# A fused add and GELU: from 1 MB tiles with stores on GpSimd's queue to uniform 512 KB chunks, x kept in SBUF, adds on GpSimd and temporaries in PSUM

## The chip, the cores and the metric

The kernel runs on one core of a Trainium2 chip. The metric is the device time of one execution in microseconds, as the median of several runs. One further execution was recorded by the hardware profiler; all views of the profile come from it.

## The reference

```python
x, y = randn(1024, 4096), randn(1024, 4096)      # float32
z = x + y
out = 0.5 * z * (1 + tanh(sqrt(2 / pi) * (z + 0.044715 * z ** 3)))   # float32
```

Two arrays of 16 MiB are read and one of 16 MiB is written: 48 MiB (50.33 MB) pass between HBM and SBUF. Each output element depends on one element of each input.

## The kernel before

The 1024 rows are viewed as 128 partitions with 8 rows each, so that one partition owns 32768 elements in a row, 128 KB of HBM. This row is cut along its length into 15 tiles of 2048 columns (1 MB for all partitions, 8 KB per partition) and a tail of 1024, 512, 256, 128 and 128 columns: 20 tiles.

For each tile, in the names of the code: `do_load` fetches a and b (lines 67 and 68, both from SyncE's queue, SP); `do_add` makes z = a + b on VectorE (DVE, line 75); `do_sq` makes w = k3 z² on ScalarE (ACT, line 81); `do_stt` makes w = (w + k1) z on VectorE (line 90); `do_ti` runs Tanh and then 0.5 w + 0.5 as an Identity, both on ScalarE (lines 100 and 105); `do_mul_store` makes w = z w on VectorE (line 116) and stores it from GpSimd's queue (POOL, line 117).

One loop at the end sets the order: in step t it emits the load of tile t, Tanh and Identity of t-3, the add of t-1, the second VectorE operation of t-2, the Square of t-1, and the product and store of t-3. The input pool has six buffers for each of a and b, the chain pool five for each of z and w. So a load waits for the add that read its buffer six tiles ago.

Of the kernel before, what the change touches and what calls it, by code (L numbers as in the profile page):

```python
# [1 line left out]

# [1 line left out]

# [4 lines left out]


@with_exitstack
def kernel(
    ctx: ExitStack,
    tc: tile.TileContext,
    x: bass.AP,
    y: bass.AP,
    out: bass.AP,
):
    nc = tc.nc  # L20
    P = nc.NUM_PARTITIONS
    fp32 = mybir.dt.float32

    N, D = x.shape
    assert N % P == 0
    rows_per_part = N // P

    k1 = math.sqrt(2.0 / math.pi)
    k3 = k1 * 0.044715
    sqrt_k3 = math.sqrt(k3)  # L30

    xv = x.rearrange("(p n) d -> p (n d)", p=P)
    yv = y.rearrange("(p n) d -> p (n d)", p=P)
    ov = out.rearrange("(p n) d -> p (n d)", p=P)

    total_free = rows_per_part * D
    FMAX = 2048

    tail = [1024, 512, 256, 128, 128]
    nbody = (total_free - sum(tail)) // FMAX  # L40
    assert sum(tail) + nbody * FMAX == total_free
    sizes = [FMAX] * nbody + tail
    offsets = []
    off = 0
    for F in sizes:
        offsets.append(off)
        off += F
    C = len(sizes)

    in_pool = ctx.enter_context(tc.tile_pool(name="inputs", bufs=6))  # L50
    chain_pool = ctx.enter_context(tc.tile_pool(name="chain", bufs=5))
    consts = ctx.enter_context(tc.tile_pool(name="consts", bufs=1))

    half = consts.tile([P, 1], fp32, tag="half")
    nc.vector.memset(half, 0.5)  # L55

    a_t: list = [None] * C
    b_t: list = [None] * C
    z_t: list = [None] * C
    w_t: list = [None] * C  # L60

    def do_load(c):
        F = sizes[c]
        sl = slice(offsets[c], offsets[c] + F)
        a = in_pool.tile([P, F], fp32, tag="a")
        b = in_pool.tile([P, F], fp32, tag="b")
        nc.sync.dma_start(out=a, in_=xv[:, sl])  # L67
        nc.sync.dma_start(out=b, in_=yv[:, sl])
        a_t[c] = a
        b_t[c] = b  # L70

    def do_add(c):
        F = sizes[c]
        z = chain_pool.tile([P, F], fp32, tag="z")
        nc.vector.tensor_add(out=z, in0=a_t[c], in1=b_t[c])  # L75
        z_t[c] = z

    def do_sq(c):
        F = sizes[c]
        w = chain_pool.tile([P, F], fp32, tag="w")  # L80
        nc.scalar.activation(  # L81
            out=w,
            in_=z_t[c],
            func=mybir.ActivationFunctionType.Square,
            scale=sqrt_k3,
        )
        w_t[c] = w

    def do_stt(c):
        nc.vector.scalar_tensor_tensor(  # L90
            out=w_t[c],
            in0=w_t[c],
            scalar=k1,
            in1=z_t[c],
            op0=mybir.AluOpType.add,
            op1=mybir.AluOpType.mult,
        )

    def do_ti(c):
        nc.scalar.activation(  # L100
            out=w_t[c],
            in_=w_t[c],
            func=mybir.ActivationFunctionType.Tanh,
        )
        nc.scalar.activation(  # L105
            out=w_t[c],
            in_=w_t[c],
            func=mybir.ActivationFunctionType.Identity,
            scale=0.5,
            bias=half,  # L110
        )

    def do_mul_store(c):
        F = sizes[c]
        sl = slice(offsets[c], offsets[c] + F)
        nc.vector.tensor_mul(out=w_t[c], in0=z_t[c], in1=w_t[c])  # L116
        nc.gpsimd.dma_start(out=ov[:, sl], in_=w_t[c])  # L117

    for t in range(C + 4):
        if 0 <= t < C:  # L120
            do_load(t)
        if 0 <= t - 3 < C:
            do_ti(t - 3)
        if 0 <= t - 1 < C:
            do_add(t - 1)
        if 0 <= t - 2 < C:
            do_stt(t - 2)
        if 0 <= t - 1 < C:
            do_sq(t - 1)
        if 0 <= t - 3 < C:  # L130
            do_mul_store(t - 3)


# [1 line left out]
_INS = ['x', 'y']  # L135
_OUTS = [((1024, 4096), 'float32')]


# [23 lines left out]
```

## Time and profile before

| | |
|---|---|
| median of 5 runs | 132.49 us (132.36 to 132.89) |
| the profiled execution's own time | 132.47 us |
| its span in the profile | 130.7 us |
| DVE busy | 107.8 us (83% of the span), 61 instructions |
| ACT busy | 96.0 us (73%), 61 instructions |
| POOL busy | 11.0 us (8%), 24 instructions |
| HBM read, written | 33.55 MB, 16.78 MB |
| packets | 8258; loads take 62.2% of the 16 engines' span, stores 30.9% |
| one 128x2048 operation | 2291 ns (L75), 1907 ns (L81), 2288 ns (L90), 1908 ns (L100), 2001 ns (L105), 2289 ns (L116) |
| one 128x1024 operation | 1222 ns (L75), 1041 ns (L81), 1224 ns (L90), 1039 ns (L100), 1132 ns (L105), 1225 ns (L116) |
| the issue of one store on POOL | 540 ns |

The span is the time between the first and the last instruction that the profiler recorded; the execution takes 1.8 us more. The page's second part shows the busy share of each engine and of the 16 DMA engines in 40 slices of 3.27 us. The view by stretches gives the same for stretches of one's own choice, and the GB/s that the DMA moved in each. The share of the DMA can come out somewhat above 1, because packets on one engine can overlap.

### The profile page before, as it was taken

The numbers are of one execution on the slowest core, as the hardware profiler recorded it, in microseconds if no ns is written. First come the engines' busy times: TensorE is split into PE (matmuls) and PEld (weight loads), VectorE is DVE, ScalarE is ACT, GpSimd is POOL, SyncE is SP. The second block draws the span as 40 slices with busy tenths as digits, with TensorE's granted clock in tenths as the row PEclk, the third lists the DMA queues.
The fourth block names the chain that finished last, engine by engine and source line by source line (L and its number), as shares of the span: only waits on it lengthen the run. The fifth ranks groups of instructions, "written<-read, shape, count | busy, mean of one in ns | idle before, by whom it ended". The sixth has DMA issues, their size and how long they took to land.

```text
span 130.7 us, 306 instructions
## 1 busy us (share of the span) xinstructions
DVE 107.8 (83%) x61; ACT 96.0 (73%) x61; POOL 11.0 (8%) x24
## 2 busy tenths in 40 slices
DVE  0053949999999999987959999996969899999930
ACT  3005592899998989894985989894885979899850
POOL 0000002001010000001010100001010100110341
DMA  4999999999999999999999999999999999817690
GB/s 140 419 424 434 424 424 426 334 421 434 424 424 431 426 426 429 421 431 431 421 429 431 419 431 434 419 431 431 419 434 431 405 401 406 335 48 321 273 339 30
DMA packets 8258, 50.35 MB, mean 385 GB/s; under 512 B 960, under 2 KB 1728, under 8 KB 2496
## 3 DMA queue, kind: packets, MB, share of 16 engines
q1 hardware_dynamic: 5760, 33.56, 62.2%
q0 software_dynamic: 2496, 16.78, 30.9%
q14 instruction: 2, 0.02, 0.0%
HBM read 33.55 MB, written 16.78 MB: 385 GB/s over the span
## 4 chain that ended last, share of the span: by engine, by line
DMA 45%; issue 43%; POOL 5%; DVE 3%; POOLq 1%; SPq 0%; DVEq 0%
DMA b<-in_y_dram 45%; POOL out_dram L117 5%; DVE w L90 2%; DVE w L116 2%; POOLq L157 0%; SPq L67 0%; POOLq L117 0%; DVE z L75 0%; DVEq L75 0%
## 5 line engine op out<-in xcount | busy, mean ns | idle before, releaser
L75 DVE TENSOR_TENSOR z<-a,b 128x2048 f32<-128x2048 f32 (+4 forms) x20 | 37.3, 1864 | 12.9 <-DMA b<-in_y_dram 12.8
L81 ACT ACTIVATE w<-z 128x2048 f32<-128x2048 f32 (+4 forms) x20 | 31.3, 1564 | 22.4 <-DVE z L75 21.9
L116 DVE TENSOR_TENSOR w<-z,w 128x2048 f32<-128x2048 f32 (+4 forms) x20 | 37.3, 1863 | 3.0 <-ACT w L105 3.0
L90 DVE SCALAR_TENSOR_TENSOR w<-w,z 128x2048 f32<-128x2048 f32 (+4 forms) x20 | 37.2, 1862 | 2.4 <-ACT w L81 2.4
L100 ACT ACTIVATE w<-w 128x2048 f32<-128x2048 f32 (+4 forms) x20 | 31.3, 1566 | 7.0 <-DVE w L90 6.9
L105 ACT ACTIVATE w<-w,half 128x2048 f32<-128x2048 f32 (+4 forms) x20 | 33.2, 1659 | 0.6
L117 POOL DMA_DIRECT2D out_dram<-w x20 | 10.8, 540 | 116.5 <-DVE w L116 114.6
L81 ACT ACT_TABLE_LOAD x1 | 1.3, 1283 | 0.7 <-PEq L146 0.7
L55 DVE MEMSET half<- 128x1 f32 x1 | 0.1, 59 | 0.8 <-PEq L146 0.8
L146 POOL MEMSET const-float32-0.0<- 128x1 f32 x1 | 0.1, 98 | 0.2 <-issue 0.2
L146 POOL MEMSET const-bfloat16-1.0<- 128x1 bf16 x1 | 0.1, 101 | 0.0
L146 POOL MEMSET const-float32-1.0<- 128x1 f32 x1 | 0.1, 98 | 0.0
L146 POOL MEMSET const-uint8-127<- 128x1 uint8 x1 | 0.1, 98 | 0.0
## 6 DMA issues: line engine op xcount, KB each, us to landing
a<-in_x_dram SPq DMA_DIRECT2D x15, 1024.0 KB, 27.5
b<-in_y_dram SPq DMA_DIRECT2D x15, 1024.0 KB, 28.5
out_dram<-w POOLq DMA_DIRECT2D x15, 1024.0 KB, 9.1
a<-in_x_dram SPq DMA_DIRECT2D x1, 512.0 KB, 28.9
b<-in_y_dram SPq DMA_DIRECT2D x1, 512.0 KB, 26.5
out_dram<-w POOLq DMA_DIRECT2D x1, 512.0 KB, 3.8
a<-in_x_dram SPq DMA_DIRECT2D x1, 256.0 KB, 23.4
b<-in_y_dram SPq DMA_DIRECT2D x1, 256.0 KB, 21.3
```

The source lines that it names most:

```text
L55: nc.vector.memset(half, 0.5)
L75: nc.vector.tensor_add(out=z, in0=a_t[c], in1=b_t[c])
L81: nc.scalar.activation(out=w, in_=z_t[c], func=mybir.ActivationFunctionType.Square, scale=sqrt_k3,)
L90: nc.vector.scalar_tensor_tensor(out=w_t[c], in0=w_t[c], scalar=k1, in1=z_t[c], op0=mybir.AluOpType.add, op1=mybir.AluOpType.mult,)
L100: nc.scalar.activation(out=w_t[c], in_=w_t[c], func=mybir.ActivationFunctionType.Tanh,)
L105: nc.scalar.activation(out=w_t[c], in_=w_t[c], func=mybir.ActivationFunctionType.Identity, scale=0.5, bias=half,)
L116: nc.vector.tensor_mul(out=w_t[c], in0=z_t[c], in1=w_t[c])
L117: nc.gpsimd.dma_start(out=ov[:, sl], in_=w_t[c])
L146: nc = _bacc.Bacc("TRN2", target_bir_lowering=False, num_devices=1)
```

## The change

The kernel is written anew for the same mathematics. 1 + tanh(u) is 2 sigmoid(2u), so that the Identity goes: w = (c z² + c1) z with doubled constants, then Sigmoid, then z times that.

- All tiles have 1024 columns: 32 chunks of 512 KB, 4 KB per partition. The view of HBM is the same, 128 KB per partition.
- Each x chunk has a buffer of its own for the whole run (32 of 4 KB per partition). The add writes z over x, and the product writes the result over z; the store reads it from there.
- y has four buffers of 4096 columns, each filled by four loads.
- The temporary w lies in PSUM[...].
- The adds of chunks 2 to 29 run on GpSimd, those of the first two and the last two on VectorE.
- All loads stay in SyncE's queue, x and y in turn. The stores move from GpSimd's queue to ScalarE's.
- The order on each engine is written out by hand, and a first Sigmoid on one column runs ahead of everything.

The new functions and the order:

```diff
+    by_pool = set(range(2, C - 2))
+    xpool = ctx.enter_context(tc.tile_pool(name="xz", bufs=1))
+    ypool = ctx.enter_context(tc.tile_pool(name="y", bufs=YB))
+    ppool = ctx.enter_context(
+        tc.tile_pool(name="w", bufs=4, space=bass.MemoryType.PSUM)
+    )
...
-        nc.sync.dma_start(out=a, in_=xv[:, sl])
-        nc.sync.dma_start(out=b, in_=yv[:, sl])
+        nc.sync.dma_start(out=xt[t], in_=hbm(x, t))
...
+        nc.sync.dma_start(out=yt[t], in_=hbm(y, t))
...
-        nc.gpsimd.dma_start(out=ov[:, sl], in_=w_t[c])
+        nc.scalar.dma_start(out=hbm(out, t), in_=xt[t])
...
-        nc.vector.tensor_add(out=z, in0=a_t[c], in1=b_t[c])
+        eng = nc.gpsimd if c in by_pool else nc.vector
+        eng.tensor_add(out=z(c), in0=z(c), in1=yt[t][:, o : o + f])
...
+        wt[c] = ppool.tile([P, CH], fp32, tag="w", name=f"w{c}")[:, :f]
+        nc.scalar.activation(out=wt[c], in_=z(c), func=act.Square, scale=root)
...
+        nc.vector.scalar_tensor_tensor(
+            out=wt[c], in0=wt[c], scalar=c1, in1=z(c), op0=alu.add, op1=alu.mult
...
+        nc.scalar.activation(out=wt[c], in_=wt[c], func=act.Sigmoid)
...
+        nc.vector.tensor_mul(out=z(c), in0=wt[c], in1=z(c))
...
+    for i in range(-3, C + 1):
+        if 0 <= i < C:
+            dve.append((stt, i))
+            acts.append((sig, i))
+        if 0 <= i - 1 < C:
+            dve.append((mul, i - 1))
+        if 0 <= i + 3 < C and i + 3 not in by_pool:
+            dve.append((add, i + 3))
+        if 0 <= i + 2 < C:
+            acts.append((sq, i + 2))
+        if 0 <= i - 3 < C:
+            acts.append((store, i - 3))
+    acts += [(store, t) for t in range(C - 2, C)]
```

In the text, sig, sq, stt, mul, add and store with a number are these functions for that chunk; load n is the n-th of the 64 loads (x of chunk 0, y of chunk 0, x of chunk 1, and so on).

## The prediction

> **What bounds the kernel now.** I read the slices first (part 2 of the page): where is the DMA row below 9?
>
> ```profile
> DMA  4999999999999999999999999999999999817690
> GB/s 140 419 424 434 424 424 426 334 421 434 424 424 431 426 426 429 421 431 431 421 429 431 419 431 434 419 431 431 419 434 431 405 401 406 335 48 321 273 339 30
> ```
>
> From the second slice to the 34th the 16 DMA engines are full; DVE is 83% busy, ACT 73%. So the body is bound by bytes: 48 MiB (50.33 MB), which neither kernel can avoid. What is not bytes lies in the first slice, in the eighth (334 GB/s) and in the last six. The stretches give sizes (columns: us, DVE, ACT, POOL busy, clock, DMA share, GB/s):
>
> ```profile
> 9.00:21.00 12.00, 8.22 (x5) 7.62 (x4) 0.00 (x0) 1.00 1.01 425
> 28.00:100.00 72.00, 66.66 (x31) 59.47 (x32) 5.32 (x10) 1.00 1.01 427
> 104.20:106.00 1.80, 1.77 (x1) 1.45 (x1) 0.50 (x1) 1.00 1.01 412
> 114.00:118.00 4.00, 4.00 (x4) 3.67 (x2) 0.53 (x1) 1.00 0.25 104
> 118.00:122.00 4.00, 4.00 (x5) 3.68 (x6) 0.53 (x1) 1.00 0.56 231
> 126.00:131.00 5.00, 0.29 (x1) 0.59 (x2) 0.54 (x1) 1.00 0.32 113
> ```
>
> Loads alone run at 425, loads and stores together at 427. From 114 us the DMA starves while DVE is busy 4.00 of 4.00 us: the last loads are in, and the stores wait for DVE's remaining work. The account of the span of 130.7 us: 50.33 MB at 427 is 117.9; the start costs 2.2 (41 GB/s in the first 2 us, 336 in the next 2, against 427); the end, after the last DMA packet at 128.7, is 2.0; 8.6 is left as lost DMA time, of which 0.7 in the eighth slice and 7.9 in the tail.
>
> The third line of the stretches matters most: from 104.2 to 106.0 almost only the 128x1024 loads (4 KB rows) are moving, and they reach 412, with the engines as full. The trace's single packets say why: one of 8192 B lasts 309 ns, one of 4096 B 159 ns, a semaphore write 9 ns, so each packet carries some 9 ns beside its bytes.
>
> [...] eight packets and a semaphore write per engine and 512 KB transfer are 8 x 159 + 9 = 1281 ns, 409 GB/s. [...] Square (1907 ns) and Tanh (1908 ns) agree. [...] before has no DMA behind an ACTIVATE, so when a store in ACT's queue is issued is not shown.
>
> **The change part by part.**
>
> *Rows.* Before has 45 transfers with 8 KB rows and 15 small ones; after has 96 of 4 KB rows. Alone: 1.281 us each. Under two queues before gained 427 over 422 (8 x 309 + 9 ns per MB); the same 1% gives 1.268. I take 1.27: 96 x 1.27 = 121.9 us, **4.0 more** than 117.9. Bounds: 120.4 (each packet gains the 3.5 ns that an 8 KB one gains, 418 GB/s) and 123.0 (no gain). The layout in HBM, 128 KB per partition, stands in both kernels; that part adds nothing.
>
> *Stores from POOL to ACT.* Removes POOL's 540 ns per issue; adds 32 issues on ACT. SP's issues take 0.33 to 0.6 us in the timeline; ACT per chunk then is 2 x 1.04 (128x1024 row) + 0.4 = 2.5 us. A chunk's bytes take 3 x 1.27 = 3.8 us: hidden. The lull in the eighth slice came with the first store (issued at 21.2, first packet at 25.7); without POOL's queue I let its 0.7 go, but keep it in the range.
>
> *Arithmetic.* Identity goes (33.2 us of ACT), Sigmoid replaces Tanh. DVE: 64 x 1.225 + 4 adds x 1.225 = 83 us[...]: 2.6 us a chunk. POOL: 28 adds[...]. All lie under the 3.8 us; this gains nothing in the body, because ACT and DVE were hidden there too. If POOL needed over 3.8 us, or if the DMA were faster, they would show.
>
> *x resident.* No load waits for a store's buffer, and y's four buffers only make the loads of chunk 16 wait for adds 0 to 3, done by 15 us. But the built queues show a new wait: loads and stores share eight DMA semaphores in turn, so each transfer waits for the one eight places ahead. Load 21 waits for store 0; store 0 stands behind the wait of Square 5, hence behind load 12 and POOL's add. At 1.281 a load, load 12 lands at 17; [...] store 0 lands by 24, and loads 13 to 20 keep the DMA busy to 27.5 or later. Covered by 3.5 us; with adds of 3.2 us or more each the cover is gone and SP stalls.
>
> *Tail.* Count from the start of add 31 on DVE (0 = last load landed). DVE starts follow each other at 1.14 to 1.2 us: add 31, stt 29, mul 28, stt 30, mul 29, stt 31, mul 30, mul 31. Ends: stt 29 at 2.4, stt 30 at 4.7, stt 31 at 7.0, mul 31 at 9.4. Store k stands on ACT behind sig k+3 and so waits for stt k+3: store 26 is issued at 2.5, store 27 at 4.7, store 28 at 7.0, 29 to 31 at 7.4, 8.2, 9.4; store 25 just before 0. Data follow 1.0 us after the issue (the first load: issued 0.74, first packet 1.74). The DMA idles 2.5 us ahead of store 26, 1.0 ahead of 27, 1.0 ahead of 28; the last four run back to back to 13. With 0.1 before store 25 the loss is 4.6; [...] if ACT issues a store only after the ACTIVATEs ahead have ended, 2 more. I take 5.3, against 7.9 before: **2.6 less**.
>
> *Start and end* as before (2.2 and 2.0); the first packet needs the same SP issue.
>
> Sum: 2.2 + 121.9 + 5.3 + 2.0 = 131.4 us, 0.7 over the span of 130.7. The profiled execution took 132.47, 1.8 over its span, and stands with the median of 132.49: **133.2 us**.
>
> **The rivals.**
> - *Faster: the row cost is hidden.* Place: the 73 or so transfers that run while both queues are full. If 4 KB packets from two queues overlap so that each 512 KB takes 1.227 us (427 GB/s), the sum falls by 73 x 0.043 = 3.1 to 130.1. It decides from about 1.257 us (417 GB/s) down, where the forecast crosses 132.5. For: shares above 1 mean that packets overlap, and from 108 to 109 us short rows beside 8 KB stores read 436 GB/s at a share of 1.10. Against: the 4 KB stretch at 412 was as full as the rest.
> - *Slower: ACT's queue is serial.* Stores are issued only behind finished ACTIVATEs: tail loss 7.3 instead of 5.3, and the start loses up to 1 us as store 0 comes late: 135.2 to 136.2. For: the stores share a queue with two ACTIVATEs per chunk. [...]
> - *Slower: POOL binds.* If an add took 4.5 us, 28 of them from 10.0 end at 136, and the tail's 15 follow: 152. [...]
> - *It does not do what it says:* the HBM layout is unchanged, so if that was the point, nothing moves; included in the main case.
>
> **How the numbers follow.** Main case 0.45 (132.3 to 134.3), hidden row cost 0.25, serial ACT queue 0.22, POOL or the shared semaphores stalling 0.08. A difference under 0.2% (0.27 us) is about what these runs can't tell from none: 132.2 to 132.8 is "same". The main case puts 0.09 there and 0.02 below; faster 0.27, same 0.09, slower 0.64. The range of 130.6 to 136.4 takes in the hidden row cost down to 0.5 above its full size and the serial queue.
>
> **What would show it.** Right: packets of 4096 B at 155 to 159 ns, 409 to 418 GB/s in the body; no SP wait on a store that empties the DMA; after the last load three gaps of the DMA that end with stt 29, 30 and 31; the last packet 13 us after add 31. Wrong: 425 GB/s or more with 4 KB rows; POOL adds over 3.2 us; holes in the DMA row before 110 us; stores issued only as the ACTIVATE ahead of them ends.

## The result and the profile after

The changed kernel takes 131.88 us (median of 28 runs, 131.52 to 132.56) against 132.52 us (47 runs) for the kernel before: a ratio of 0.9959 with a 95% interval of 0.9950 to 0.9969. It is 0.4% faster. The forecast was 133.2 us, 0.5% slower, and gave faster a chance of 0.27.

The slices of the changed kernel's page, to be laid beside those of before:

```profile
DMA  4999999999999999999999999999999999943594
GB/s 133 395 397 419 414 408 408 382 422 422 420 422 422 420 415 419 422 420 417 419 420 422 419 420 420 415 418 418 419 419 419 422 414 419 413 188 161 215 407 182
```

The body is as full as before and moves fewer bytes a second, around 420. The tail is still there, in the slices with 188, 161 and 215. The view by stretches gives sizes (us, DVE, ACT, POOL busy, clock, DMA share, GB/s):

```profile
2.00:4.00 2.00, 0.00 (x0) 0.21 (x2) 0.00 (x0) 1.00 0.95 334
4.00:10.00 6.00, 2.65 (x3) 1.20 (x2) 0.00 (x0) 1.00 1.02 398
24.00:27.00 3.00, 2.80 (x3) 2.45 (x3) 2.24 (x1) 1.00 1.01 385
30.00:100.00 70.00, 42.60 (x37) 36.17 (x38) 42.21 (x18) 1.00 1.03 420
113.00:116.00 3.00, 2.26 (x3) 1.94 (x2) 0.00 (x0) 1.00 0.87 352
116.00:119.00 3.00, 3.00 (x3) 0.76 (x1) 0.00 (x0) 1.00 0.05 18
119.00:122.00 3.00, 3.00 (x4) 2.19 (x3) 0.00 (x0) 1.00 0.66 265
122.00:125.00 3.00, 3.00 (x3) 1.01 (x1) 0.00 (x0) 1.00 0.69 276
```

The same account as in the prediction, for both profiled executions:

| us | before | forecast | after |
|---|---|---|---|
| start, beyond the bytes moved in it | 2.2 | 2.2 | 2.3 |
| bytes, with the holes up to 30 us | 118.6 | 121.9 | 120.7 |
| tail: DMA time lost; for before what is left of the span, for after from 113 us | 7.9 | 5.3 | 5.8 |
| from the last DMA packet to the end | 2.0 | 2.0 | 1.6 |
| sum, and the span in the profile | 130.7 | 131.4 | 130.4, span 130.6 |

For after, 50.33 MB at 420 GB/s are 119.8 us, and the slower stretches up to 30 us (398, 414, 408, 385 and 416 GB/s in the trace) add 0.9. The tail: 352, 18, 265, 276, 404 and 107 GB/s in six stretches of 3 us are 10.2 us of transfers at 420, in the 16.0 us from 113 to the last packet at 128.96. Counted in the same way, before loses 7.3 us from 111 to its last packet at 128.7; the other 0.6 of its 7.9 is spread over the stretches ahead.

So in the two profiles the smaller rows cost 2.1 us, the tail gives back 1.5 to 2.1 (by which of the two counts one takes), and the end gives 0.4. The two spans differ by only 0.1 us, because the profiled execution of the changed kernel is one of its slower ones, 132.33 us.

The engines have room in the body. These are the costliest groups of the changed kernel's page (busy time, mean ns of one, idle time before and what ended it):

```profile
L91 POOL TENSOR_TENSOR x<-x,y 128x1024 f32<-128x1024 f32 x28 | 65.7, 2346 | 43.3 <-DMA y<-in_y_dram 43.2
L99 DVE SCALAR_TENSOR_TENSOR w<-w,x 128x1024 f32<-128x1024 f32 x32 | 39.4, 1232 | 31.4 <-ACT w L96 31.3
L107 DVE TENSOR_TENSOR x<-w,x 128x1024 f32<-128x1024 f32 x32 | 38.9, 1216 | 0.5 <-ACT w L104 0.5
L104 ACT ACTIVATE w<-w 128x1024 f32<-128x1024 f32 x32 | 31.5, 985 | 8.3 <-DVE w L99 7.4
```

GpSimd's adds take 2346 ns and wait 43 us for loads: GpSimd does not bind. And the tail in the order of time, with lines left out (ACTq is ScalarE's instruction queue):

```profile
114.01 0.34 ACTq L82 DMA_DIRECT2D out_dram<-x  x1
115.83 1.23 DVE L91 TENSOR_TENSOR x<-x,y 128x1024 f32<-128x1024 f32 x1 [0.74 <-DMA y<-in_y_dram]
116.98 1.23 DVE L99 SCALAR_TENSOR_TENSOR w<-w,x 128x1024 f32<-128x1024 f32 x1
118.24 1.01 ACT L104 ACTIVATE w<-w 128x1024 f32<-128x1024 f32 x1 [2.29 <-DVE w L99]
118.24 0.34 ACTq L82 DMA_DIRECT2D out_dram<-x  x1
119.16 1.02 ACT L96 ACTIVATE w<-x 128x1024 f32<-128x1024 f32 x1
120.51 0.34 ACTq L82 DMA_DIRECT2D out_dram<-x  x1
122.77 2.90 ACTq L82 DMA_DIRECT2D out_dram<-x  x4
```

Add 31 starts at 115.83. Stores 26, 27 and 28 are issued 2.4, 4.7 and 6.9 us later, each as stt 29, 30 and 31 ends; store 25 stands at 114.01. Two ACTIVATEs stand ahead of store 26 on ScalarE: sig 29 (L104), which starts at 118.24, and the Square of chunk 31 (L96), which starts at 119.16. The store goes out at 118.24, before the Square has started and before sig 29 has ended, so it does not wait until the ACTIVATEs ahead of it end. But the store does not pass an ACTIVATE that still waits: its product was ready at 106.6 (VectorE's L107 of chunk 26), and it left only when stt 29, which ended at 118.21, had released sig 29.

### The profile page after: what moved, and what is told of

It reads as the page before. It is cut to its first block, busy times and chain, and to the rows that moved or that the text cites. A ratio compares the mean times of both kernels' runs of the same rounds, so it can differ in the third digit from the quotient of the medians.

```text
span 130.6 us, 345 instructions
## 1 busy us (share of the span) xinstructions
DVE 80.0 (61%) x69; ACT 64.0 (49%) x66; POOL 65.9 (50%) x32
## 4 chain that ended last, share of the span: by engine, by line
DMA 81%; DVE 7%; POOL 4%; SPq 3%; issue 1%; POOLq 0%; DVEq 0%; ACT 0%
DMA y<-in_y_dram 41%; DMA x<-in_x_dram 30%; DMA out_dram<-x 10%; POOL x L91 4%; DVE x L107 3%; DVE w L99 3%; SPq L72 2%; SPq L79 1%; DVE x L91 1%; POOLq L91 0%; DVEq L91 0%; ACT w L96 0%
## 5 line engine op out<-in xcount | busy, mean ns | idle before, releaser
L91 POOL TENSOR_TENSOR x<-x,y 128x1024 f32<-128x1024 f32 x28 | 65.7, 2346 | 43.3 <-DMA y<-in_y_dram 43.2
L99 DVE SCALAR_TENSOR_TENSOR w<-w,x 128x1024 f32<-128x1024 f32 x32 | 39.4, 1232 | 31.4 <-ACT w L96 31.3
L96 ACT ACTIVATE w<-x 128x1024 f32<-128x1024 f32 x32 | 32.9, 1027 | 50.7 <-POOL x L91 44.2
L107 DVE TENSOR_TENSOR x<-w,x 128x1024 f32<-128x1024 f32 x32 | 38.9, 1216 | 0.5 <-ACT w L104 0.5
L104 ACT ACTIVATE w<-w 128x1024 f32<-128x1024 f32 x32 | 31.5, 985 | 8.3 <-DVE w L99 7.4
L91 DVE TENSOR_TENSOR x<-x,y 128x1024 f32<-128x1024 f32 x4 | 4.9, 1225 | 12.3 <-DMA y<-in_y_dram 12.3
```

Source lines behind the costliest of these rows:

```text
L91: eng.tensor_add(out=z(c), in0=z(c), in1=yt[t][:, o : o + f])
L96: nc.scalar.activation(out=wt[c], in_=z(c), func=act.Square, scale=root)
L99: nc.vector.scalar_tensor_tensor(out=wt[c], in0=wt[c], scalar=c1, in1=z(c), op0=alu.add, op1=alu.mult)
L104: nc.scalar.activation(out=wt[c], in_=wt[c], func=act.Sigmoid)
L107: nc.vector.tensor_mul(out=z(c), in0=wt[c], in1=z(c))
```

## The experiments

All versions are timed against the kernel before on the same chip, which there took 132.59 to 132.69 us (132.46 in the one execution beside the kernels of transfers alone).

**8 KB rows in the changed kernel.** Transfers of two chunks, computation as it was:

```diff
-    sizes = [CH] * (TOT // CH)
+    sizes = [2 * CH] * 13 + [CH] * 6
...
+    tile_of = {c: t for t, c in last.items()}
...
-        if 0 <= i - 3 < C:
-            acts.append((store, i - 3))
+        if i - 3 in tile_of:
+            acts.append((store, tile_of[i - 3]))
```

> The changed kernel with 13 transfers of 2048 columns (8 KB rows) and 6 of 1024 per array; computation still in chunks of 1024. Theory A (each packet costs a fixed 9 ns and, with both queues full, gains some 3 to 3.5 ns back by overlap, so a 4 KB row costs 1.250 against 1.227 us per 512 KB): body rate from 420 to 426 or 427 GB/s, 78 x 0.023 = 1.8 us less, less up to 0.5 for coarser stores: 130.1 to 130.6 us. Theory B (the recorded step: 1.27 us per 512 KB of 4 KB rows): 78 x 0.043 = 3.4 us less, 128.5. Theory C (the body rate of 420 comes from something other than rows, such as the shared semaphores or reads and writes in turn): rate stays at 420, time within 0.3 of 131.9.

Measured: 129.26 us, ratio 0.9755 (0.9735 to 0.9775). The stretch of its body:

```profile
30.00:100.00 70.00, 46.05 (x41) 38.65 (x40) 44.45 (x20) 1.00 1.01 426
```

426 is theory A's rate; C falls. At these rates bytes take 1.7 us less (50.33 MB at 426 and at 420), as A has it. The time missed all three: it lies between A's 130.1 and B's 128.5, and the median fell by 2.6. In the two profiles, whose spans differ by 3.4, the tail lost about 4.7 us instead of 5.8, and the end after the last packet was 1.2 instead of 1.6. Neither was expected.

Rows and transfer size change together here and in all runs below (8 KB rows with 1 MB, 4 KB rows with 512 KB). The semaphore write of a transfer takes 9 ns on each engine, its eight packets 8 x 159 ns, so the difference is put to the packets; no run changes one without the other.

**4 KB rows in the kernel before.**

```diff
-    FMAX = 2048
+    FMAX = 1024
...
-    in_pool = ctx.enter_context(tc.tile_pool(name="inputs", bufs=6))
-    chain_pool = ctx.enter_context(tc.tile_pool(name="chain", bufs=5))
+    in_pool = ctx.enter_context(tc.tile_pool(name="inputs", bufs=12))
+    chain_pool = ctx.enter_context(tc.tile_pool(name="chain", bufs=10))
```

> The kernel before with tiles of 1024 columns (4 KB rows) and the pools' buffer counts doubled, so that the same bytes are in flight; the tail sizes stand. Theory A (4 KB rows cost 1.250 us per 512 KB under two queues, whichever queues): body rate 419 to 420, 2.1 us more of DMA, less 0 to 2 us because the last full tiles are half as long: 132.5 to 134.6. Theory B (1.27): body rate 412 to 414, 134.4 to 136.4. Theory C (the gain of the changed kernel needs both queues to be hardware queues, and GpSimd's stores lack it): body rate 409 to 414 as in B.

Measured: 133.10 us, ratio 1.0032 (1.0019 to 1.0044). Its body, with the stores still on GpSimd:

```profile
30.00:100.00 70.00, 64.77 (x57) 60.84 (x57) 10.10 (x19) 1.00 1.03 419
```

So 4 KB rows run at 419 to 420 in both kernels, whichever queue stores. The recorded 1.27 us per 512 KB (413 GB/s) was too dear, and which pair of queues it is does not matter.

This run also shows what the small tiles do to the tail. From 111 us to its last packet at 128.3 it loses 5.3 us (410, 391, 287, 194, 223 and 178 GB/s in six stretches of 3 us), against 7.3 in the kernel before. So the small tiles alone (with the buffer counts doubled) bring both the dearer rows and the shorter tail, with the Identity still there and all adds still on VectorE. Between this kernel and the changed one lie 1.2 us (133.10 and 131.88), and what differs by as much in the traces is the end after the last packet: 2.8 us here, 1.6 there. The changed kernel's tail is not shorter (5.8); in the two profiles, where it is the longer by 0.5, the spans differ by 0.6.

**Transfers alone.** Three kernels without arithmetic, with rows of 8, 4 and 2 KB in turn. The loads and the stores of the three:

```diff
 # one queue
+        nc.sync.dma_start(out=xt[t], in_=xv[:, sl])
+        nc.sync.dma_start(out=b, in_=yv[:, sl])
+        nc.sync.dma_start(out=ov[:, sl], in_=xt[t])          # after all loads
 # two queues
+        nc.scalar.dma_start(out=b, in_=yv[:, sl])
+        (nc.sync if t % 2 else nc.scalar).dma_start(out=ov[:, sl], in_=xt[t])
 # side by side: loads on sync, store(t - 2) in step t
+        nc.scalar.dma_start(out=ov[:, sl], in_=xt[t])
```

> No arithmetic: x and y are loaded and x is stored as it is, so the output is x; columns in transfers of 2048 (8 KB rows), then 1024, then 512 (2 KB rows); all transfers in SyncE's queue, all stores behind all loads. Packet sum with no overlap (8192 B 309 ns, 4096 B 159 ns, 2048 B 86 ns, semaphore 9 ns, 8 packets and a semaphore per engine): 422.6, 409.3 and 376 GB/s in the three stretches of loads, and the same for stores if reads and writes cost alike. If single-queue packets overlap as well, 1 to 2.4% more.

> As the kernel with one queue, but x is loaded by SyncE and y by ScalarE, and the stores alternate between the two queues, still behind all loads of their queue: two queues of loads without stores, then two queues of stores without loads. Theory A (two queues save 3 to 3.5 ns per packet, whatever they move): 427, 419 and 392 GB/s. Theory B (a fixed 1%): 427, 413, 380. Theory C (the gain comes from reads beside writes): the single queue's 423, 409, 376.

> As above, loads in SyncE's queue, each store in ScalarE's as soon as its x has landed: loads and stores side by side. Theories A and C: 427, 419 and 392 GB/s. Theory B: 427, 413, 380. In the stretch of 2 KB rows the shared semaphores leave eight transfers of 0.67 us in flight and may leave holes; only full stretches count there.

One profiled execution each, of 128.91, 128.56 and 131.07 us. Stretches of the kernel with one queue (columns: us, POOL busy, clock, DMA share, GB/s; first the loads of 8, 4, 2 KB, then the stores of 8, 4, 2 KB):

```profile
5.00:29.00 24.00, 0.00 (x0) 1.00 1.01 423
35.00:55.00 20.00, 0.00 (x0) 1.00 1.03 410
60.00:82.00 22.00, 0.00 (x0) 1.00 1.06 387
84.00:94.00 10.00, 0.00 (x0) 1.00 1.03 427
102.00:109.00 7.00, 0.00 (x0) 1.00 1.02 419
114.00:124.00 10.00, 0.00 (x0) 1.00 1.06 406
```

The kernel with two queues, the same stretches of loads:

```profile
5.00:29.00 24.00, 0.00 (x0) 1.00 1.01 425
35.00:55.00 20.00, 0.00 (x0) 1.00 1.03 410
60.00:82.00 22.00, 0.00 (x0) 1.00 1.06 387
```

Its stores run at 430, 420 and 406. Loads and stores side by side, 8, 4 and twice 2 KB:

```profile
12.00:40.00 28.00, 0.00 (x0) 1.00 1.01 427
52.00:80.00 28.00, 0.00 (x0) 1.00 1.03 420
89.00:92.00 3.00, 0.00 (x0) 1.00 1.05 389
92.00:124.00 32.00, 0.00 (x0) 1.00 1.04 385
```

Two queues give loads nothing: 410 and 410, 387 and 387. Theories A and B fall. Stores run faster than loads at equal rows (419 against 410 at 4 KB), and at 8 and 4 KB loads beside stores run at the stores' rate, as C has it. At 2 KB they do not (389 and 385; stores alone 406), so that C's figure of 392 is missed there, as is the 376 that the packet sum without overlap had for loads of 2 KB rows alone. For 4 KB rows the numbers stand: 410 for loads alone, 420 for loads beside stores, without a second queue as the reason.

The single packets of these traces show where the difference lies. In the loads alone the 4096 B packets last 159 to 172 ns, 163 in the mean, with one queue and with two. In the stores alone they last 159, and with loads and stores side by side 159.1 in the mean, in both queues. The DMA share is 1.02 to 1.03 in all of these stretches, so packets overlap equally with one queue and with two. Why a load's packet lasts longer when no store runs beside it is open. It is not fixed either, since the first loads of some kernels (4 to 10 us) ran at 419 to 421 before falling to 408 to 411.

**The last stores behind the last load.** In SyncE's queue, which has nothing to do once the loads are issued:

```diff
-        nc.scalar.dma_start(out=hbm(out, t), in_=xt[t])
+        eng = nc.sync if t >= M else nc.scalar
+        eng.dma_start(out=hbm(out, t), in_=xt[t])
...
+    M = 22
...
-        if 0 <= i - 3 < C:
+        if 0 <= i - 3 < M:
             acts.append((store, i - 3))
-    acts += [(store, t) for t in range(C - 2, C)]
+    sp += [(store, t) for t in range(M, T)]
```

> The changed kernel with the stores of chunks 22 to 31 in SyncE's queue, behind the last load, instead of in ScalarE's. Theory A (the tail's lost DMA time of 5.8 us comes from stores that stand in ScalarE's queue behind waits for stt 28 to 31 while earlier stores were served ahead of the last loads): the last load lands some 3.7 us earlier (112 instead of 115.8), stores 22 to 27 fill the DMA while DVE works off the last chunks, lost tail time near 1 us, 127.0 to 128.0 us. Theory B (the tail is bound by DVE's eight operations after the last load, wherever the stores stand): the last load lands when it did, gain at most 1 us, 131 us or more.

Measured: 127.88 us, ratio 0.9641 (0.9629 to 0.9654). Add 31 starts at 112.90 instead of 115.83, and the stretches of its tail are

```profile
111.00:114.00 3.00, 3.00 (x3) 1.94 (x2) 0.00 (x0) 1.00 1.04 418
114.00:117.00 3.00, 3.00 (x4) 1.71 (x2) 0.00 (x0) 1.00 1.03 419
117.00:120.00 3.00, 3.00 (x4) 1.43 (x3) 0.00 (x0) 1.00 0.93 381
120.00:123.00 3.00, 2.08 (x2) 0.82 (x1) 0.00 (x0) 1.00 0.72 288
```

The DMA works at full rate while DVE works off the last chunks: lost tail time is 1.5 us, near what theory A has (about 1).

Two things changed in it: ten stores come after the loads, and they leave ScalarE's waits. With M = 27 only the last five do so, and as many stores as in the changed kernel are still to come when the last load lands:

> As the kernel with the last stores in SyncE's queue, but only those of chunks 27 to 31; stores 24 to 26 stand on ScalarE behind the waits for stt 27 to 29 as in the changed kernel. Theory A (what counts is how many stores are still to come when the last load lands: here as many as in the changed kernel): the last load lands at 115 to 116 us, tail loss falls only by what stores 27 to 29 gain by leaving ScalarE's queue, the last packet 12.1 instead of 13.1 us after add 31: 130.5 to 131.3 us. Theory B (what counts is that stores leave ScalarE's queue): near the 127.9 of the kernel with ten such stores, 129 or less.

Measured: 131.03 us, ratio 0.9886 (0.9865 to 0.9908). Add 31 starts at 115.24, the last packet ends 12.2 us later. Theory A holds. When the last load's packets end, 6.9 transfers are still to come in the changed kernel, 7.0 here and 10.0 with M = 22. For the last stores leaving ScalarE's queue is worth 0.9 us (131.88 to 131.03); having three more left over for the tail is worth 3.1 us (131.03 to 127.88), in which the share of store 26 leaving ScalarE's queue too is not separated.

**Stores on GpSimd in the changed kernel.**

```diff
-        nc.scalar.dma_start(out=hbm(out, t), in_=xt[t])
+        nc.gpsimd.dma_start(out=hbm(out, t), in_=xt[t])
...
+    for c in range(C + 6):
         if c in by_pool:
             pool.append((add, c))
+        if 0 <= c - 6 < C:
+            pool.append((store, c - 6))
```

(The stores in ScalarE's order are removed.)

> The changed kernel with its stores issued by GpSimd, store c-6 behind add c, the last ones as their products end. Stores no longer stand behind ScalarE's waits nor share semaphores with the loads. Theory A (rows alone set the body rate; the tail is set by what stores are left when the last load lands and by DVE's eight operations): body rate 419 to 420, last packet within 1 us of the changed kernel's, end later by 0.4 to 1.2 us: 131.5 to 133.0 us. Theory B (two hardware queues are needed for 420): body 410 to 414, 133.5 to 135. Theory C (ScalarE's queue was the tail's loss, whatever the lag): tail loss down by 3 us or more, 129 us or less.

Measured: 130.14 us, ratio 0.9806 (0.9781 to 0.9831), between A and C. Body and tail:

```profile
30.00:100.00 70.00, 44.66 (x39) 36.42 (x38) 53.01 (x37) 1.00 1.03 419
117.00:120.00 3.00, 3.00 (x4) 1.92 (x2) 0.91 (x2) 1.00 0.78 314
120.00:123.00 3.00, 2.76 (x3) 1.01 (x1) 0.68 (x2) 1.00 0.45 182
123.00:126.00 3.00, 0.00 (x0) 0.00 (x0) 0.53 (x1) 1.00 0.86 343
```

The body is 419 once more, so B falls. The last load lands earlier than A had it: add 31 starts at 113.57, because the stores of chunks 23 to 26 come out only at 107.8 and after, behind GpSimd's last add. More stores are left over (8.3 transfers instead of 6.9), DMA stays full to 117 us, and the tail loses 2.9 us instead of 5.8. Queue and place of the stores change together in this run. The end is later, as expected: 2.5 us after the last packet instead of 1.6.

**Stores on ScalarE in the kernel before.**

```diff
-        nc.gpsimd.dma_start(out=ov[:, sl], in_=w_t[c])
+        nc.scalar.dma_start(out=ov[:, sl], in_=w_t[c])
```

> The kernel before with its stores issued by ScalarE instead of GpSimd, at the same place in the loop. Theory A (the queue matters only at the edges: the end after the last packet falls from 2.0 to about 1.6 us, the lull ahead of the first store stays since the changed kernel has one as well; ScalarE waits at most 0.5 us a step for the product, with 7.4 us of transfers a step): body rate 427 as before, 132.0 to 132.5 us. Theory B (GpSimd's descriptors cause the lull of 0.7 us and a later end): 131.4 to 131.8. Theory C (ScalarE's blocking for the product of the same step stalls the chain): slower than 133.

Measured: 140.79 us, ratio 1.0612 (1.0590 to 1.0633): theory C. The longest entry of its waits (engine, line, waited for: us in total, times, longest us):

```profile
ACT w L105 <- DVE w L116: 19.1, 8, 7.2
```

ScalarE stands up to 7.2 us at a store for the product of the same step, and the Identity queued behind it stands with it. The body still moves 426 GB/s from 30 to 100 us. What falls behind is the computation (the last 128x2048 product starts at 125.7 us instead of 118.5), and the bill comes when the loads have landed: 5 GB/s from 111 to 114 us, 25 from 117 to 120. But the loads stand as well. In the kernel before, SyncE's loads never wait for a store; here they wait 22.2 us in three waits (the same columns):

```profile
SPq L67 <- DMA out_dram<-w: 11.8, 2, 8.5
SPq L68 <- DMA out_dram<-w: 10.4, 1, 10.4
```

A late load delays VectorE's add, and with it the product behind it that ScalarE waits for: at 65.4 us an add has waited 5.1 us for its load, and the store that ScalarE stands at goes out at 69.9, after the product behind that add. How much of the 8.2 us comes from ScalarE's block and how much from these waits no run separates. In the changed kernel's order each store stands behind the waits of sig k+3, long after its product, and its body stays full. That this order is what keeps it full is argued, not tested.

**The changed kernel once more.**

> The changed kernel itself, one more profile. Its runs fall into two groups, 131.5 to 131.9 and 132.1 to 132.6, and the profiled one is of the upper. That profile shows 396 GB/s from 4 to 10 us where kernels with the same start show 419, 0.3 us. If that hole makes the groups, a run of the lower group has 415 or more there; if not, the rate there and the group are unrelated.

Measured: 131.88 us, of the lower group. Its stretches:

```profile
2.00:4.00 2.00, 0.00 (x0) 0.22 (x2) 0.00 (x0) 1.00 0.79 283
4.00:10.00 6.00, 2.78 (x3) 1.33 (x2) 0.00 (x0) 1.00 1.03 421
24.00:27.00 3.00, 2.81 (x3) 2.44 (x3) 2.12 (x1) 1.00 1.03 412
```

Neither the hole of 398 nor that of 385 is there, and 421 is what the expectation asks for. But the account does not close. Against the first profile this one gains 0.3 us from 4 to 10 and 0.2 from 24 to 27 us, and it loses 0.2 from 2 to 4 (283 GB/s against 334) and 0.1 from 10 to 20 (408 against 414). At 30 us it is 0.2 ahead, of the 0.45 between the two executions; the rest comes later (add 31 at 115.39 instead of 115.83). That the hole makes the groups is not shown, and what makes the holes is open.

**Together.** Both edits, rows and last stores:

> Both edits together: 8 KB rows for the first 26 chunks and the stores from chunk 22 on in SyncE's queue. If rows (theory A there) and tail (theory A there) add up: 125.3 to 126.5 us. If the tail is bound by DVE's work: about that of rows8 alone.

Measured: 126.15 us, ratio 0.9511 (0.9497 to 0.9525). That is inside the expectation. Alone the edits gained 2.6 and 4.0 us, together 5.7, which is the 1.7 us of the bytes and the 4.0 of the tail; what the rows gained beside their bytes does not come on top. With stores held back from chunk 20 on:

> The best version so far (8 KB rows for 26 chunks, last stores in SyncE's queue), with two more chunks' stores held back: from chunk 20 on. It still lost 1.6 us of DMA time after the last load; two more chunks held back are 2.4 us of transfers to fill it. If that loss is a lack of ready stores: 0.5 to 1.2 us less than 126.15, 125.0 to 125.6. If it is the wait for the last products: the same within 0.3.

Measured: 125.77 us, ratio 0.9476 (0.9459 to 0.9494), just outside both expectations. Its tail is full to 120 us (423, 429, 410, 419 GB/s in stretches of 3 us from 108 on); in this profile a hole of 393 GB/s from 20 to 30 us hides part of the gain. It is the fastest version, 5.2% under the kernel before.

## Why the prediction was wrong

- **The step that failed: "I take 1.27".** Rows of 4 KB do cost, but 512 KB at 420 GB/s are 1.25 us per transfer. The 96 transfers came to 120.7 us with the holes, not 121.9. The bound of 120.4 was in the text; the value taken lay between it and no gain at all, on the ground that 1% of overlap with two queues carries over as 1%. The ground was wrong too: two queues of loads gain nothing, and 1.25 comes with loads beside stores. My rate of 412 for 4 KB rows was read from loads alone, and the 409 is the sum of their packets; loads alone are under a fifth of the work.
- **A sum that fitted by luck.** "Alone: 1.281" took 159 ns for a packet and no overlap, and its 409 GB/s all but met the 410 of loads alone. There the packets last 163 ns in the mean, which gives 399 GB/s without overlap, and they overlap by 3%: two errors that cancel. Beside stores the packet does last 159, and the same overlap gives the 420.
- **The end** was 1.6 instead of 2.0 us, a term I had left unchanged although the queue that ends last was changed.
- **The tail** came out 0.5 us larger than taken. Its mechanism was right in detail: stores 26 to 28 at 2.4, 4.7 and 6.9 us after add 31 (forecast 2.5, 4.7, 7.0), the last packet at 13.1 (forecast 13). The size is in part luck: the 5.3 stood 0.7 us above the gaps counted (4.6), an allowance, mostly for slower reads of PSUM, that rested on no trace. No slower reads came (VectorE's operations with w in PSUM took 1232 and 1216 ns, against 1224 and 1225 in SBUF), while stores 26, 27 and 28, each alone on the DMA for nearly all of its time, took 1.43 to 1.44 us from first to last packet where 1.25 is the rate of the body.
- These sum to -1.2 - 0.4 + 0.5 + 0.1 (start) = -1.0 us with the rounded terms, where the spans differ by 0.8. The profiled execution took 132.33, 0.45 over its kernel's median, so that the forecast was 1.3 us above the median. With a forecast difference of 0.7 us, terms of this size decide the sign.
- **The rivals.** "The row cost is hidden" named 417 GB/s as the point from which it decides, and 420 came. By the prediction's own sum the point is 1.260 us or 416 GB/s (0.7 us over 73 transfers). The rival was right in direction, and not in size: it put 4 KB rows at 427, and they do cost. Its reason (overlap of two queues) was wrong. The serial ScalarE queue did not show: stores go out as the ACTIVATE that held them starts (118.24 and 118.24, 120.51 and 120.50, 122.77 and 122.76 us). GpSimd did not bind, at 2346 ns an add; the forecast counted on an add time that no trace of before showed.
- **The shared semaphores** were nearer than forecast. Store 0 was issued at 21.2, its first packet came at 24.9 and load 21 was issued at 28.1, after a wait of 5.2 us for it, where I had the store landed by 24 (which rested on the same add time). The DMA stayed at 416 GB/s from 27 to 30 us, so the cover held, barely.
- **Costed at nothing, rightly:** the Identity removed, the adds moved to GpSimd and the issues on ScalarE. ScalarE fell from 96 to 64 us busy and DVE from 107.8 to 80.0, with no mark on the body: the kernel before with 4 KB rows, which has none of the three, runs its body at 419 too. The lull that I had put to GpSimd's first store belongs to no queue: the kernel before shows 363 GB/s from 24 to 27 us with its stores on ScalarE as well, against 333.
- **Slips without weight.** An 8 KB packet gains 3.2 ns by the text's own rates (25 ns over 8 packets), not 3.5, which makes the bound 120.5. The waits of y's loads for adds come at chunks 20, 24 and 28 as well as 16.

## What to carry to other kernels

In a kernel bound by transfers, price a change in row length from a stretch where loads and stores run as they will run, not from loads alone (with 4 KB rows 420 and 410 GB/s here). Engine time that was freed in the body brought nothing here; what was left to win lay in the tail, and there the question is how many stores are still to come when the last load lands: held back behind the last loads in an idle queue they fill the time in which the last chunks are computed (4.0 us here). A store in a computing engine's queue cost little where it stood far behind its product (0.9 us for the last ones). Where it stood right behind it the kernel took 8 us more, the loads' waits for stores included.

## What was not expected of the hardware

- Loads of 4 KB rows alone ran at 410 GB/s, stores alone at 419, both together at 420; with 2 KB rows 387, 406 and 385 to 389. The mean packet of 4096 B lasted 163 ns in loads alone and 159 in the other two. A second queue changed none of the single rates by more than 3 GB/s.
- The time from the last packet to the end of the span differs by kernel: 2.0 us before, 1.3 with its stores on ScalarE, 2.8 with twice the tiles, 2.5 with GpSimd's stores in the changed kernel, 1.6 with ScalarE's, 1.2 with fewer and larger transfers.
- VectorE's operations with one input in PSUM took 1232 and 1216 ns, where those with all operands in SBUF took 1224 and 1225: a slower read of PSUM did not show.
- In the kernel before, with 8 KB rows, the loads slow down just before the first store's packets appear at 25.7 us: 333 GB/s from 24 to 27. The changed kernel with such rows shows 380 from 27 to 30. With 4 KB rows it slowed down in one profile of two (385 and 412 GB/s from 24 to 27), and with its last stores held back it did not (414 with M = 22, 411 with M = 27).
